# A two-layer mLSTM and conformer trunk on one core: modulation products dealt out, norm 1 without GpSimd, a fourth convolution block on VectorE, and tile starts made equal modulo 64

## The chip, the cores and the metric

The kernel runs on one core of one Trainium2 chip. The metric is the device time of one execution in microseconds; lower is better. Engines are named as in the profile: PE is TensorE (PEld its weight loads), DVE is VectorE, ACT is ScalarE, POOL is GpSimd, SP issues nearly all DMA transfers. Each engine works through its own queue in order.

## The reference

One sequence of 1024 positions and 1024 channels passes two layers. Layer 0 mixes with an mLSTM, layer 1 with a causal conformer convolution; each is followed by a gated ConvFFN (1024 to 2 x 2816 and back). Each sub-layer has a norm that is modulated by a conditioning vector.

```python
c_act = jax.nn.silu(c)
for layer in range(DEPTH):                                   # DEPTH = 2
    mod = c_act @ ada_w[layer] + ada_b[layer]                # 1024 -> 6 * 1024
    sh1, sc1, g1, sh2, sc2, g2 = jnp.split(mod, 6, axis=-1)
    h = modulate(rmsnorm(x, norm_mix_g[layer]), sh1, sc1)
    # layer 0: mlstm_block (w_up 1024 -> 2 * 2048, 4-tap conv, 4 heads, w_down 2048 -> 1024)
    # layer 1: conformer_conv_block:
    #   a, gte = split(h @ w_pw1 + b_pw1); u = a * sigmoid(gte)
    #   u = causal_dwconv(u, dw_w, dw_b)  (31 taps); u = silu(layernorm(u)); y = u @ w_pw2 + b_pw2
    x = x + g1[:, None, :] * y
    h = modulate(rmsnorm(x, norm_ffn_g[layer]), sh2, sc2)
    x = x + g2[:, None, :] * conv_ffn(h, ffn_w_up[layer], ffn_conv_w[layer], ffn_conv_b[layer], ffn_w_down[layer])
return rmsnorm(x, final_g)
```

## The kernel before

**Data and products.** Channels lie on the 128 partitions, positions along the free side, in two halves of 512 (`h` is 0 or 1). A product in fp32 is made of three passes over rounded parts: `split` writes a rounded copy on ACT (L172) and the remainder by a subtract on DVE (L173; on POOL where it is given that engine). `proj` (L201) is one output block of 128 channels for one half: 8 blocks x 3 passes = 24 products. The z half of the mLSTM's up projection and the ConvFFN's matrices use a seven-product form in the manner of Strassen (`Forms`, `Seven`, L468), whose operands are sums of quarters, made on DVE, and whose outputs are combined on DVE and ACT (L564 to L583).

**What sets the order.** A scheduler orders the instructions of each engine from the program's order and priorities and from the tile pools; each engine then runs its queue in order. A tile that is used again makes its next writer wait for its last reader, a DMA writer too.

**The stages** in order of time: norm 1 of layer 0; the x half of the up projection with the 4-tap convolution and the q, k, v maps per block i (16 blocks, `post`); the z half per block j (8); the chunkwise attention; `mlstm_down`, which keeps `residual` steps (L463) for 8 output blocks and both halves and forms the next norm; ConvFFN of layer 0 (up per j, then down); the conformer; ConvFFN of layer 1; the final norm.

**Modulation.** `mod` has 96 columns of 128 channels. Each takes a DMA of 512 KB into a tile `ada` and one DVE operation (`ada_block`, L155: multiply by `crep`, the replicated conditioning vector, and sum), then an add of the bias (L156, one column). 16 of them stand in norm 1, two per i in the x half, ten per j in the z half; all are done before attention. `scale_of` (L161) forms the scale of a norm.

**Norm 1** (`FirstNorm`): the squares of half 0 are summed on PE by a matrix of ones (L310), those of half 1 by adds on POOL (L312) and one product. `apply` scales (L326), maps on ACT (L328, L329) and subtracts (L330), with DVE for half 0 and POOL for half 1.

**The conformer.** `order` gives the projections of pw1. For each block j, `glu` makes the gated u. The blocks j < ON_PE are convolved on DVE (`conv_dve`, L1655: 31 steps of multiply and add, put into a list `slow`, from which `filler(RATE)` takes RATE steps after each projection); the others on PE (`conv_pe`, L1633, with banded weights `wband`, 36 products per half block). For PE's blocks `glu` writes `cU` (L1606), `spread` copies it to `u_d` in DRAM and back as `u`, in four phases. The last four blocks (TAIL) have their projections split by half. `layer_norm` is a generator that `steps` moves on.

Of the kernel before, what the change touches and what calls it, by code (L numbers as in the profile page):

```python
# [15 lines left out]
P = 128  # L16
# [17 lines left out]
EPS = 1e-6  # L34
BIG = 1.0e30
# [31 lines left out]
for _name, _w in (("ident", P), ("posmask", P), ("mask4", 32), ("sel16", 8)):  # L67
    CON[_name] = (_n, _w)
    _n += _w
NCON = _n  # L70
ON_PE = 3
TAIL = 4
LPC = -100
RATE = 5
# [3 lines left out]
def trunk(ctx, tc, a):  # L78
# [50 lines left out]
    epst = main.tile([P, 1], F32, name="epst")  # L129
# [21 lines left out]
    def ada_block(layer, b):  # L151
        crep, pool, bufs = ada_
        w = pool.tile([P, D], F32, tag="ada", name=nm("ada"), bufs=bufs)
        dma(w, a["ada"][layer, b])
        v.scalar_tensor_tensor(w, w, 1.0, crep, ALU.mult, ALU.mult, accum_out=mod[:, layer, b : b + 1])  # L155
        v.tensor_tensor(mod[:, layer, b : b + 1], mod[:, layer, b : b + 1], pv("ada_b", layer, b), ALU.add)  # L156
# [7 lines left out]

    def ada_part(layer, part):
        for k in range(KB):
            ada_block(layer, 8 * part + k)
        if part in (1, 4):
            scale_of(layer, part // 3, 0, KB)
# [129 lines left out]
    class FirstNorm(Norm):  # L299
        def stats(self, h):  # L300
# [5 lines left out]
            for k in range(KB):  # L306
                s = t512()
                sc.activation(s, self.x[:, k, sl], AF.Square)
                if not h:
                    pe.matmul(o, ones, s, start=k == 0, stop=k == KB - 1)  # L310
                elif k:
                    gp.tensor_tensor(acc, acc, s, ALU.add)  # L312
                else:
                    acc = s
            if h:
                pe.matmul(o, ones, acc, start=True, stop=True)
            self.r[h] = inverse_rms(o)

        def apply(self, h, k):
# [6 lines left out]
            (v, gp)[h].tensor_tensor(xs, xs, self.r[h], ALU.mult)  # L326
# [3 lines left out]
            (v, gp)[h].tensor_tensor(hl[:, 1], xs, hl[:, 0].bitcast(F32), ALU.subtract)  # L330
# [116 lines left out]
    def conv_tile(pool, nk):  # L447
        u = pool.tile([P, nk - 1 + S], F32, tag="u", name=nm("u"), bufs=3)
        gp.memset(u[:, : nk - 1], 0.0)
        return u  # L450

    def causal_conv(pool, u, o, h, taps, bias, nk, bufs):
        c0 = h * HS
        sc.copy(u[:, nk - 1 + c0 : nk - 1 + c0 + HS], o)
        c = pool.tile([P, HS], F32, tag="c", name=nm("c"), bufs=bufs)
        sc.activation(c, o, AF.Identity, scale=taps[nk - 1], bias=bias)
        for i in range(nk - 2, -1, -1):
            v.scalar_tensor_tensor(c, u[:, i + c0 : i + c0 + HS], taps[i], c, ALU.mult, ALU.add)
        return c
# [130 lines left out]
    class Operands:  # L590
# [39 lines left out]
        def forms(self, j):  # L630
            b11, b2, t13, t42 = t512(), raw_tile(), raw_tile(self.extra, 2), raw_tile(self.extra, 2)
# [30 lines left out]
    def ffn_up(layer, normed, p_d, hx, ux, es_u, other, ops):  # L662
# [13 lines left out]
        def channel(b, pool=ux):  # L676
            u[b] = pool.tile([P, FK - 1 + S], F32, tag="u", name=nm("u"), bufs=2 + (pool is ux))
# [92 lines left out]
        ops.extra = rx  # L770
# [161 lines left out]
    def mlstm(normed, x0, keep, k1, es1, es_x0):  # L932
# [6 lines left out]
        if True:  # L939
# [4 lines left out]
            g2 = k1.tile([P, IB, 9], F32, name="g2")  # L944
            g1r = k1.tile([P, 2, IB, 8], F32R, name="g1r")
# [8 lines left out]
            ws.load(1, tag="wux", pool=ada_[1], bufs=1, ahead=0, engine=gp)  # L954
            ws.load(lead, ahead=0, engine=gp)
# [37 lines left out]
            ada_[1:] = k1, 2  # L993
            es_x0.close()
            ADAX, ADAZ = 2, 10
            T1_AT, T1_ENG = IB - 2, v
            with ExitStack() as es_z:
# [3 lines left out]
                def post(j, u, xc, xr):  # L1001
# [12 lines left out]
                    bv = mp.tile([P, 137], F32, tag="bv", name=nm("bv"))  # L1014
# [856 lines left out]
```

## Time and profile before

| | us |
|---|---|
| median of 3 runs | 2717.94 (2715.34 to 2719.88) |
| the profiled execution | 2718.93 |
| its span | 2717.0 |

| engine | busy us | share |
|---|---|---|
| PE | 2558.2 | 94% |
| DVE | 2207.1 | 81% |
| ACT | 1353.5 | 50% |
| POOL | 253.5 | 9% |

Stages by the trace: start to 135 us (loads, norm 1, first projections), x half to about 300, z half to 480, attention to 745, mlstm_down to 925, the norm behind it to 991, ConvFFN 0 up to 1372 and down to 1538, conformer to 2016, norm to 2083, ConvFFN 1 up to 2470 and down to 2637, end at 2717. Read the lines so: a group's "mean ns of one" is the duration of one instruction, and the idle time shown with it is that of its engine just before it; a wait's columns are the total, the number and the longest. An engine's idle time matters only where the end of the program hangs on it.

### The profile page before, as it was taken

To read this page: it belongs to the slowest core of one execution; us is meant where nothing else is said; L and a number is where in the kernel's file an instruction comes from. 1 tells how busy PE (TensorE), PEld (TensorE's weight loads), DVE (VectorE), ACT (ScalarE), POOL (GpSimd) and SP (SyncE) were. 2 spreads that over 40 slices of the span, in tenths; PEclk is the share of its full clock that TensorE was granted. 3 is DMA by queue.
4 is the path that set the end of the run, shared out by engine and by line. 5 is a ranking of instruction groups with operands and counts; after the bars stand their busy time and mean duration, and the time that the engine had idled before them with its cause. 6 is when DMAs were issued, how large, how long until landed. Compare 5 with 4: busy or idle time off the path is not lost.

```text
span 2717.0 us, 31936 instructions
## 1 busy us (share of the span) xinstructions
PE 2558.2 (94%) x11565; PEld 2072.4 (76%) x11565; DVE 2207.1 (81%) x3026; ACT 1353.5 (50%) x2085; POOL 253.5 (9%) x338
## 2 busy tenths in 40 slices
PE   4899898999999989999999999799998999999998
PEld 2788676788878768888877888778776788887787
DVE  7999998787767899898898679923489888988866
ACT  4654443777634544444444342466764444445424
POOL 5311254333100000000000000000000000000000
PEclk7999999999999989999999999899998999999999
DMA  7576465532387323233264342444332223326422
GB/s 254 180 244 227 142 209 202 194 119 96 132 282 230 120 101 116 104 110 112 92 219 146 101 144 66 136 159 159 143 119 101 109 102 113 109 89 225 140 80 99
DMA packets 150526, 395.68 MB, mean 146 GB/s; under 512 B 14880, under 2 KB 37600, under 8 KB 150368
## 3 DMA queue, kind: packets, MB, share of 16 engines
q1 hardware_dynamic: 150368, 393.64, 42.2%
q8 instruction: 91, 1.49, 0.2%
q14 instruction: 67, 0.55, 0.1%
HBM read 301.28 MB, written 92.31 MB: 145 GB/s over the span
## 4 chain that ended last, share of the span: by engine, by line
PE 60%; DVE 13%; DMA 4%; ACT 3%; issue 2%; SPq 0%; POOL 0%; DVEq 0%; ACTq 0%; POOLq 0%
PE ps L468 36%; PE ps L201 15%; DVE cy L1655 4%; DVE h L173 3%; PE ps L1381 3%; PE ps L1418 2%; PE ps L1633 2%; DVE wu L173 1%; DVE c L778 1%; DVE x L736 1%; DMA raw<-xc_d 1%; PE ps L1558 1%; DMA raw<-t_d 1%; PE ps L1363 1%; DMA raw<-in_fdownS 0%
## 5 line engine op out<-in xcount | busy, mean ns | idle before, releaser
L468 PE MATMUL ps<-h,wu 128*128 128x512 f32 x4704 | 1121.0, 397 | 42.9 <-ACT wu L172 11.6
L468 PEld LDWEIGHTS ps<-h,wu 128*128 128x128 f32 x4704 | 890.9, 190 | 259.2 <-ACT wu L172 13.7
L201 PE MATMUL ps<-h,wu 128*128 128x512 f32 (+1 forms) x2478 | 574.5, 389 | 1.2 <-DVE wu L173 1.1
L201 PEld LDWEIGHTS ps<-h,wu 128*128 128x128 f32 x2478 | 458.9, 189 | 99.9 <-issue 3.3
L172 ACT CAST wu<-raw 128x1024 fp32r<-128x1024 f32 (+1 forms) x286 | 297.8, 1044 | 285.3 <-PE ps L201 93.4
L173 DVE TENSOR_TENSOR wu<-raw,wu 128x1024 fp32r<-128x1024 f32 (+1 forms) x266 | 322.7, 1214 | 89.2 <-ACT wu L172 88.1
L778 DVE SCALAR_TENSOR_TENSOR c<-u,par,c 128x1024 f32<-128x1024 f32 x176 | 220.9, 1279 | 4.9 <-ACT c L776 4.0
L776 ACT ACTIVATE c<-u,par 128x1024 f32<-128x1024 f32 x88 | 108.9, 1244 | 147.4 <-DVE u L579 130.6
L468 PE MATMUL ps<-h,w 128*128 128x512 f32 x672 | 169.2, 399 | 1.9 <-ACT w L172 1.8
L468 PEld LDWEIGHTS ps<-h,w 128*128 128x128 f32 x672 | 127.5, 190 | 34.0 <-ACT w L172 2.7
L155 DVE SCALAR_TENSOR_TENSOR ada<-ada,crep 128x1024 f32<-128x1024 f32 x96 | 130.6, 1367 | 24.4 <-DMA ada<-in_ada 24.3
L463 DVE SCALAR_TENSOR_TENSOR x<-ps,mod,x 128x512 f32<-128x512 f32 (+1 forms) x140 | 98.0, 714 | 60.0 <-PE ps L201 39.5
L173 DVE TENSOR_TENSOR h<-raw,h 128x512 fp32r<-128x512 f32 (+1 forms) x188 | 124.0, 700 | 25.0 <-ACT h L172 24.8
L172 ACT CAST h<-raw 128x512 fp32r<-128x512 f32 (+1 forms) x188 | 105.8, 606 | 66.7 <-DMA raw<-p_d 26.6
L678 POOL MEMSET u<- 128x2 f32 x88 | 8.5, 100 | 1316.0 <-DVE c L778 716.5
L1381 PE MATMUL ps<-q,h 128*128 128x512 f32 (+2 forms) x576 | 116.0, 350 | 0.3 <-DVE q L173 0.3
L1655 DVE SCALAR_TENSOR_TENSOR cy<-cu,par,cy 128x1024 f32<-128x1024 f32 (+1 forms) x120 | 115.3, 1019 | 1.2 <-ACT cy L1651 0.3
L1633 PE MATMUL ps<-u,wband 128*128 128x128 f32 x720 | 91.3, 293 | 21.0 <-DMA u<-u_d 21.0
L700 ACT ACTIVATE c<-c 128x1024 f32<-128x1024 f32 x44 | 46.7, 1061 | 125.9 <-DVE c L778 125.8
L1633 PEld LDWEIGHTS ps<-u,wband 128*128 128x128 f32 x720 | 90.3, 209 | 23.5 <-issue 20.9
L1381 PEld LDWEIGHTS ps<-q,h 128*128 128x128 f32 x576 | 94.4, 188 | 17.1 <-ACT t L1446 2.0
L1642 ACT ACTIVATE cy<-ps,dwb 32x128 f32<-32x128 f32 x160 | 77.5, 485 | 38.1 <-PE ps L1633 35.8
(272 smaller groups left out, 3371.7 us busy)
## 6 DMA issues: line engine op xcount, KB each, us to landing
ada<-in_ada SPq DMA_DIRECT2D x96, 512.0 KB, 3.9
raw<-in_fup SPq DMA_DIRECT2D x94, 512.0 KB, 3.3
p_d<-c SPq DMA_DIRECT2D x44, 512.0 KB, 2.7
wband<-in_w SPq DMA_DIRECT2D x36, 576.0 KB, 4.7
raw<-in_pw SPq DMA_DIRECT2D x40, 512.0 KB, 3.4
raw<-in_mup SPq DMA_DIRECT2D x32, 512.0 KB, 4.4
raw<-t_d SPq DMA_DIRECT2D x32, 512.0 KB, 4.7
raw<-in_fdownS SPq DMA_DIRECT2D x32, 512.0 KB, 4.3
```

The source lines that it names most:

```text
L155: v.scalar_tensor_tensor(w, w, 1.0, crep, ALU.mult, ALU.mult, accum_out=mod[:, layer, b : b + 1])
L172: sc.copy(out_hi, raw)
L173: (engine or v).tensor_tensor(out_lo, raw, out_hi.bitcast(F32), ALU.subtract)
L201: pe.matmul(o, t[:, i, c : c + P], acts[k][:, j, :], start=k == 0 and n == 0, stop=k == nk - 1 and n == 2,)
L463: v.scalar_tensor_tensor(xs, o, gate, xs, ALU.mult, ALU.add)
L468: pe.matmul(o, w[:, i, k * P : (k + 1) * P], acts[k][:, j, :], start=first and k == 0 and q == 0, stop=last and k == n - 1 and q == 2, ski ...
L776: sc.activation(c, body(b), AF.Identity, scale=taps[FK - 1], bias=pv("fcb", layer, b))
L778: v.scalar_tensor_tensor(c, u[b][:, i : i + S], taps[i], c, ALU.mult, ALU.add)
L1381: pe.matmul(so[:, tlo:], xr[cc][I // nJ][:, i, I % nJ * P : (I % nJ + 1) * P], un["qs"][cc][:, j, tlo:], start=n == 0, stop=n == 3 * CB - 1,)
L1633: pe.matmul(o, wd[:, 4 * d : 4 * d + 4, :].rearrange("p d c -> p (d c)"), phases[j][:, g, n0 + d : n0 + d + N4], start=d == 0, stop=d == 8,)
L1642: sc.activation(y4[32 * g : 32 * g + 32, 3 - q, n0 : n0 + N4], o[32 * q : 32 * q + 32], AF.Identity, bias=dwb4[32 * q : 32 * q + 32, 4 * j ...
L1655: v.scalar_tensor_tensor(y, u[:, t + c0 : t + c1], pv("dww", t, j), y, ALU.mult, ALU.add)
```

## The change

1. **Modulation dealt out.** `ada_product` and `ada_bias` are apart; the bias is added for several columns at once. 16 products stay in norm 1; then 1 per i in the x half, 3 per j in the z half (layer 0's are then done), 28 of layer 1's in `mlstm_down` (one per residual of the stream, 12 in the loop after it, through a single tile), and 20 in ConvFFN 0's up projection (two per j below 4, then one, through the second tile of `ops.extra`; the first holds `crep`, reloaded from DRAM). The pool `m3` has 13 buffers for 15.
2. **Norm 1 and weights without POOL.** Half 1's squares are summed on PE as well, `apply` uses DVE for both halves, and the splits of the first four weights and of the z half's forms j >= 2 move from POOL to DVE.
3. **4-tap convolution** once per block over 1024 columns, after both halves, instead of twice over 512.
4. **Conformer:** ON_PE 4, RATE 6. Blocks 2 and 3 are convolved by halves, their second halves after `filler(-1)`. Each `conv_pe` stands after both projections of the next block instead of between them, and takes one half. `wband` loads are issued by POOL. `layer_norm` yields once more.
5. **Equal offsets:** odd-sized tiles (`epst`, `bv`, `u`, `cu`, `gb2`, `dwb4`, `sel16`) are padded to multiples of 64 bytes, so that all SBUF tiles start at the same place modulo 64.

On PE in the conformer, where the products of block 4, half 0 of the convolution stand (`ps_13505` to `ps_13547` before), between the last products of the first projection of block 5 (`ps_13475`) and the first of its second (`ps_13574`):

```order
L201 MATMUL ps_13475<-h_12548,wu_13425 128x512 x3
L201 MATMUL ps_13475<-h_12553,wu_13425 128x512 x3
L1633 MATMUL ps_13505<-u_1996_13455,wband_13415 128x128 x9
L1633 MATMUL ps_13519<-u_1996_13455,wband_13417 128x128 x9
L1633 MATMUL ps_13533<-u_1996_13455,wband_13419 128x128 x9
L1633 MATMUL ps_13547<-u_1996_13455,wband_13421 128x128 x9
L201 MATMUL ps_13574<-h_12449,wu_13472 128x512 x3
```

After, on PE, the same four stand behind the second projection of block 5 (`ps_13231`), ahead of block 6 (`ps_13343`):

```order
L219 MATMUL ps_13231<-h_12386,wu_13191 128x512 x3
L219 MATMUL ps_13231<-h_12391,wu_13191 128x512 x3
L1644 MATMUL ps_13256<-u_1933_13173,wband_13163 128x128 x9
L1644 MATMUL ps_13270<-u_1933_13173,wband_13165 128x128 x9
L1644 MATMUL ps_13284<-u_1933_13173,wband_13167 128x128 x9
L1644 MATMUL ps_13298<-u_1933_13173,wband_13169 128x128 x9
L219 MATMUL ps_13343<-h_12287,wu_13228 128x512 x3
```

They moved back by one projection of 24 products. On DVE before, the gated tile of block 4, half 0 (`cU_13457`) stands behind the whole of the second block's steps (`cy_12801`, 31 of 1024) and most of what goes with them:

```order
L1655 SCALAR_TENSOR_TENSOR cy_12802<-cu_13066,par,cy_12802 128x512
L1655 SCALAR_TENSOR_TENSOR cy_12801<-cu_12927,par,cy_12801 128x1024
L1606 SCALAR_TENSOR_TENSOR cU_13457<-ps_13273,par,t_1995_13453 128x128x4
L1655 SCALAR_TENSOR_TENSOR cy_12802<-cu_13066,par,cy_12802 128x512
L173 TENSOR_TENSOR wu_13571<-raw_13569,wu_13571 128x1024
L1655 SCALAR_TENSOR_TENSOR cy_12802<-cu_13066,par,cy_12802 128x512 x5
L173 TENSOR_TENSOR wu_13618<-raw_13616,wu_13618 128x1024
L1655 SCALAR_TENSOR_TENSOR cy_12802<-cu_13066,par,cy_12802 128x512 x27
L1606 SCALAR_TENSOR_TENSOR cU_13603<-ps_13475,par,t_2013_13599 128x128x4
```

After, on DVE, `cU_13175` is that tile, and `cy_12639` and `cy_12640` are the second and third block:

```order
L1666 SCALAR_TENSOR_TENSOR cy_12640<-cu_12911,par,cy_12640 128x512
L1666 SCALAR_TENSOR_TENSOR cy_12639<-cu_12768,par,cy_12639 128x1024
L1618 SCALAR_TENSOR_TENSOR cU_13175<-ps_13102,par,t_1932_13171 128x128x4
L1666 SCALAR_TENSOR_TENSOR cy_12639<-cu_12768,par,cy_12639 128x1024
L191 TENSOR_TENSOR wu_13228<-raw_13226,wu_13228 128x1024
L1666 SCALAR_TENSOR_TENSOR cy_12639<-cu_12768,par,cy_12639 128x1024
L1666 SCALAR_TENSOR_TENSOR cy_12640<-cu_12911,par,cy_12640 128x512
```

It stands in the middle of the second block's steps now, with fewer of them ahead of it. On SP in `mlstm_down` after, the modulation tiles stand among the weights (`in_mdown`) and the spilled tiles; before, there are none here:

```order
L156 DMA ada_6319<-in_ada 128x1024
L1497 DMA raw_6436<-hn_d_143 128x512
L200 DMA raw_6446<-in_mdown 128x1024
L1498 DMA raw_6436<-xc_d_111 128x512
L1497 DMA raw_6512<-hn_d_144 128x512
L156 DMA ada_6324<-in_ada 128x1024
L1498 DMA raw_6512<-xc_d_112 128x512
L1499 DMA t_1012_6589<-sz_d_129 128x512
L200 DMA raw_6522<-in_mdown 128x1024
L1499 DMA t_1021_6665<-sz_d_130 128x512
L156 DMA ada_6329<-in_ada 128x1024
```

Each `ada` here writes the tile that the one before it wrote, so what stands behind it on SP waits for the product of the one before.

The diff, cut to its core:

```diff
-ON_PE = 3
+ON_PE = 4
 TAIL = 4
+WIDE = 2
-RATE = 5
+RATE = 6
...
-    epst = main.tile([P, 1], F32, name="epst")
+    epst = main.tile([P, 16], F32, name="epst")[:, 0:1]
...
+    def ada_product(layer, b):
+        crep, take = ada_
+        w = take()
         dma(w, a["ada"][layer, b])
         v.scalar_tensor_tensor(w, w, 1.0, crep, ALU.mult, ALU.mult, accum_out=mod[:, layer, b : b + 1])
+    def ada_bias(layer, b0, b1):
+        ...
+        v.tensor_tensor(m, m, par[:, o + b0 : o + b1], ALU.add)
+    def adas(layer, n):
+        some = blocks_left[layer][:n]
+        del blocks_left[layer][:n]
+        for l, b in some:
+            ada_product(l, b)
+        if some:
+            ada_bias(layer, some[0][1], some[-1][1] + 1)
...
-                if not h:
-                    pe.matmul(o, ones, s, start=k == 0, stop=k == KB - 1)
-                elif k:
-                    gp.tensor_tensor(acc, acc, s, ALU.add)
...
+                pe.matmul(o, ones, s, start=k == 0, stop=k == KB - 1)
...
-            (v, gp)[h].tensor_tensor(xs, xs, self.r[h], ALU.mult)
+            v.tensor_tensor(xs, xs, self.r[h], ALU.mult)
...
-            ws.load(1, tag="wux", pool=ada_[1], bufs=1, ahead=0, engine=gp)
-            ws.load(lead, ahead=0, engine=gp)
+            ws.load(1, tag="wux", pool=xp, bufs=1, ahead=0)
+            ws.load(lead, ahead=0)
...
-                    c = causal_conv(mp, us[i], o, h, taps, pv("mcb", i), MK, 3)
...
+                    sc.copy(us[i][:, MK - 1 + h * HS : MK - 1 + (h + 1) * HS], o)
                     if h == NHALF - 1:
+                        sc.activation(xc, u[:, MK - 1 :], AF.Identity, scale=pv("mcw", MK - 1, i), bias=pv("mcb", i))
+                        for t in range(MK - 2, -1, -1):
+                            v.scalar_tensor_tensor(xc, u[:, t : t + S], pv("mcw", t, i), xc, ALU.mult, ALU.add)
...
-                        adas(ADAX)
+                        adas(0, 1)
...
-                    pairs[j] = Forms(a["mup"][IB + j], a["mup"][IB + KB + j], z1, gp if j >= 2 else None)
+                    pairs[j] = Forms(a["mup"][IB + j], a["mup"][IB + KB + j], z1)
...
-                    if j < KB - 1:
-                        adas(ADAZ)
+                    adas(0, 3)
...
+            if j < FB - 1:
+                adas(1, 2 if j < 4 else 1)
...
-        with phase("m3", 15) as mp:
+        with phase("m3", 13) as mp:
+            crep = mp.tile([P, D], F32, name="crep1", bufs=1)
+            dma(crep, crep_d)
+            ada_[:] = crep, ada_tiles(mp, 1)
...
                 residual(o, gate(i), i, h * HS)
+                adas(1, 1)
...
+                    if m < KB - 2:
+                        adas(1, 1)
...
-                dma(w, a["w4"][j - ON_PE, g])
+                gp.dma_start(w, a["w4"][j - ON_PE, g])
...
-                    us[j] = cp.tile([P, CK - 1 + S], F32, tag="cu", name=nm("cu"), bufs=3)
+                    us[j] = cp.tile([P, S + LINE], F32, tag="cu", name=nm("cu"), bufs=4)
...
                 o = proj(*normed_at(h, n))
                 filler(RATE)
+                og = proj(*normed_at(h, n + 1))
                 while ready:
                     ready.pop(0)()
                 bands(j)
-                og = proj(*normed_at(h, n + 1))
...
                     filler(-1)
-                    slow.append(conv_dve(ON_PE - 1, HS, S))
+                    slow += [conv_dve(i, HS, S) for i in range(WIDE, ON_PE)]
```

More of the change, by code (lines that the diff above doesn't have):

```diff
@@ L149, in raw_tile, with ada_block, ada_tiles @@
         return pool.tile([P, 1024], F32, tag="raw", name=nm("raw"), bufs=bufs)
-    def ada_block(layer, b):
-        crep, pool, bufs = ada_
-        w = pool.tile([P, D], F32, tag="ada", name=nm("ada"), bufs=bufs)
+    def ada_product(layer, b):
+        crep, take = ada_
+        w = take()
         dma(w, a["ada"][layer, b])
         v.scalar_tensor_tensor(w, w, 1.0, crep, ALU.mult, ALU.mult, accum_out=mod[:, layer, b : b + 1])
-        v.tensor_tensor(mod[:, layer, b : b + 1], mod[:, layer, b : b + 1], pv("ada_b", layer, b), ALU.add)
+    def ada_bias(layer, b0, b1):
+        o, _ = PAR["ada_b"]
+        o += 48 * layer
+        m = mod[:, layer, b0:b1]
+        v.tensor_tensor(m, m, par[:, o + b0 : o + b1], ALU.add)
+    def ada_block(layer, b):
+        ada_product(layer, b)
+        ada_bias(layer, b, b + 1)
+    def ada_tiles(pool, bufs):
+        return lambda: pool.tile([P, D], F32, tag="ada", name=nm("ada"), bufs=bufs)
+    blocks_left = [[(0, b) for b in range(16, 48)], [(1, b) for b in range(48)]]
+    def adas(layer, n):
[5 more added lines that the diff above has]
+            ada_bias(layer, some[0][1], some[-1][1] + 1)
     def scale_of(layer, which, k0, k1):
@@ L163, in scale_of @@
         )
[L165 to L169, printed above, removed]
     def split(raw, out_hi, out_lo, engine=None):
@@ L447, in conv_tile @@
     def conv_tile(pool, nk):
-        u = pool.tile([P, nk - 1 + S], F32, tag="u", name=nm("u"), bufs=3)
+        u = pool.tile([P, S + LINE], F32, tag="u", name=nm("u"), bufs=3)[:, : nk - 1 + S]
         gp.memset(u[:, : nk - 1], 0.0)
         return u
[L452 to L459, printed above, removed]
     def residual(o, gate, m, c0):
@@ L769, in ffn_up @@
         rx = es_u.enter_context(phase(nm("rx"), side=other))
-        ops.extra = rx
+        ops.extra = [lambda t=t: rx.tile([P, 1024], F32, tag=t, name=nm(t)) for t in ("ra", "rb")]
+        if blocks_left[1]:
+            ada_[:] = ops.extra[0](), ops.extra[1]
+            dma(ada_[0], crep_d)
         more = single(rx, "w1", 1)
@@ L800, in ffn_up @@
                 s.ready = set()
+            if j < FB - 1:
+                adas(1, 2 if j < 4 else 1)
+                if layer == 0 and not blocks_left[1]:
+                    scale_of(1, 0, 0, KB)
+                    scale_of(1, 1, 0, KB)
             for n, q in enumerate(ORDER):
@@ L944, in mlstm @@
             g2 = k1.tile([P, IB, 9], F32, name="g2")
+            sel16 = k1.tile([P, 48], F32, name="sel16")
+            dma(sel16, a["sel16"])
             g1r = k1.tile([P, 2, IB, 8], F32R, name="g1r")
@@ L1555, in layer_norm @@
                 v.scalar_tensor_tensor(at[j], om, -1.0 / D, at[j], ALU.mult, ALU.add)
+            yield
+            ov = ps()
+            for j in range(KB):
                 t = t512()
@@ L1748, in trunk @@
     x0 = xp.tile([P, KB, S], F32, name="x0")
-    ada_[:] = crep, xp, 5
+    crep_d = dpool.tile([P, D], F32, name="crep_d")
+    dma(crep_d, crep)
+    ada_[:] = crep, ada_tiles(xp, 5)
     for k in range(0, KB, 2):
```

115 lines of the change are left out of this document (50 added, 65 removed).

## The prediction

> **What bounds the kernel now.** I read the page's busy line first, then a table of busy time by stage, then what TensorE (PE) waited for, and last the groups and the timeline in the stages where PE stands.
>
> ```profile
> PE 2558.2 (94%) x11565; PEld 2072.4 (76%) x11565; DVE 2207.1 (81%) x3026; ACT 1353.5 (50%) x2085; POOL 253.5 (9%) x338
> ```
>
> PE is busy 94% of the 2717.0 us span, so almost every microsecond that leaves must be PE work that vanishes, PE work that gets shorter, or one of the few stretches in which PE stands. The table shows where those are (columns: stretch, length, busy time and count of PE, PEld, DVE, ACT, POOL, granted clock, DMA share, GB/s).
>
> ```profile
> 0.00:135.00 135.00, 88.92 (x341) 64.66 (x342) 114.91 (x187) 72.94 (x112) 62.99 (x61) 0.86 0.61 216
> 135.00:300.00 165.00, 164.54 (x815) 138.78 (x813) 158.60 (x344) 82.33 (x146) 33.24 (x58) 1.00 0.71 232
> 300.00:480.00 180.00, 153.40 (x618) 117.66 (x618) 161.95 (x248) 69.31 (x100) 71.45 (x37) 0.95 0.53 182
> 745.00:925.00 180.00, 177.73 (x769) 143.38 (x768) 129.11 (x168) 79.89 (x113) 0.17 (x3) 1.00 0.70 235
> 925.00:991.00 66.00, 51.84 (x195) 37.90 (x193) 59.77 (x83) 36.84 (x55) 0.33 (x4) 0.92 0.16 56
> 991.00:1372.00 381.00, 380.31 (x1656) 312.74 (x1657) 340.88 (x398) 178.83 (x216) 3.71 (x37) 0.99 0.32 114
> 1700.00:1944.00 244.00, 217.72 (x1206) 181.30 (x1204) 113.21 (x136) 150.80 (x267) 0.36 (x4) 0.94 0.46 155
> ```
>
> PE is idle 46.1 us in the start (0 to 135), 26.6 in the z half (300 to 480), 14.2 at the first FFN's norm and 26.3 in the conformer's second part. In the x half (135 to 300) and in the first FFN's up projection it is idle 0.5 and 0.7: there, taking work off VectorE (DVE) is worth nothing. The waits name the releasers.
>
> ```profile
> PE ps L1633 <- DMA u<-u_d: 21.0, 6, 8.9
> PE ps L201 <- ACT h L328: 16.9, 3, 11.7
> PE ps L201 <- DVE h L330: 11.9, 5, 3.1
> PE ps L468 <- DVE zv L571: 10.0, 4, 5.7
> PE ps L310 <- ACT t L308: 9.7, 1, 9.7
> PE ps L468 <- ACT zg L564: 5.3, 2, 3.3
> ```
>
> The first is the conformer's banded convolution, the lines on L201 and L310 are norm 1, those on zv and zg are the z half's combinations.
>
> **Norm 1 without GpSimd (POOL).** The groups give the prices.
>
> ```profile
> L173 POOL TENSOR_TENSOR wu<-raw,wu 128x1024 fp32r<-128x1024 f32 x20 | 55.4, 2780 | 59.6 <-ACT wu L172 59.6
> L326 POOL TENSOR_TENSOR x<-x,t 128x512 f32<-128x512 f32 x8 | 15.9, 2026 | 8.1 <-DVE t L218 8.1
> L330 DVE TENSOR_TENSOR h<-x,h 128x512 fp32r<-128x512 f32 x8 | 10.2, 1270 | 0.0
> L173 DVE TENSOR_TENSOR h<-x,h 128x512 fp32r<-128x512 f32 x56 | 36.3, 683 | 0.0
> L173 DVE TENSOR_TENSOR wu<-raw,wu 128x1024 fp32r<-128x1024 f32 x260 | 317.0, 1220 | 85.3 <-ACT wu L172 84.3
> L1558 PE MATMUL ps<-t,ones 128*128 128x512 f32 x32 | 16.8, 684 | 5.3 <-ACT t L1557 5.3
> ```
>
> One subtract of 512 takes DVE 0.683 us where POOL is quiet and 1.270 in norm 1, where POOL works beside it. The change gives DVE 16 such operations (10.9 us) and about 3 lead weight splits (3.7 us), and takes the interference away: the eight L330 alone get back 8 x (1.270 - 0.683) = 4.7. The second half's statistic becomes seven more fp32 products, 14 records at 16.8/32 = 0.53, 7.4 us of PE, in a stretch where PE stands 46 us. The modulation products of this stage stay 16. From the row of the start, DVE is 85% busy, so more work on it costs the chain unless interference falls by as much. The L156 rows below say that it does. The bounds: nothing (7.4 of PE and 14.6 of DVE eat the relief), and half of the 46.1 idle, since the loads of the first 20 us stay. I take -12, nearer the smaller end, because between 60 and 100 us PE already runs nearly without gaps.
>
> **Modulation and splits in the z half.** Before, ten products L155 with ten adds L156 stand in each j; after, three products and one add.
>
> ```profile
> L155 DVE SCALAR_TENSOR_TENSOR ada<-ada,crep 128x1024 f32<-128x1024 f32 x96 | 130.6, 1367 | 24.4 <-DMA ada<-in_ada 24.3
> 200.00:250.00 50.00, 1.56 (x11) 1.00 0.72 234
> 350.00:400.00 50.00, 8.12 (x12) 0.97 0.60 208
> ```
>
> The last two rows are L156 alone, an add of one column: 0.14 us each in the x half, where POOL does little, 0.68 each in the z half, where POOL splits weights. In a stage row DVE is 90% busy in z. It loses 32 products (48 to 16) at 1.37, 43.7 us, and about 41 adds at 0.14 to 0.68, 6 to 28 us; it gains POOL's splits, 18 x 1.22 + 6 x 0.68 = 26 us, and every remaining operation runs uninhibited. Net -24 to -46 of 162. DVE then is about 70% busy, and the wait for zv (10.0) should go, that for zg (5.3) shrink. PE's idle of 26.6 is the end that the gain can't pass; nothing is the other end, since the splits now stand in DVE's queue ahead of combinations on which PE waits. I take -20: the DVE queue is shortened by more than PE's idle.
>
> On that inhibition the Trainium skill ("SBUF — State Buffer", Two separate sides) says that VectorE and GpSimd take one port pair by an exclusive lock and the loser blocks for the whole instruction. The trace agrees: an add of one column takes five times its time beside POOL. By the rule alone, all of it would vanish with POOL's work; the eight POOL operations on L1056 that stay would keep some.
>
> **The x half.** One product per i instead of two, and the convolution per 1024 columns: all DVE and ACT work under PE that is idle 0.5 us. Taken at nothing; the cover is PE itself. What could cost is that the convolution now starts only after the second half: PE then reads xr later, but one i later anyway. 0 to +5.
>
> **Where the products go.** Of layer 1's 48, 28 move to mlstm_down and 20 to the first FFN's up projection, each with 512 KB.
>
> ```profile
> 770.00:800.00 30.00, 29.49 (x127) 23.21 (x127) 20.52 (x30) 8.90 (x13) 0.00 (x0) 1.00 0.93 329
> ada<-in_ada SPq DMA_DIRECT2D x96, 512.0 KB, 3.9
> wband<-in_w SPq DMA_DIRECT2D x36, 576.0 KB, 4.7
> ```
>
> In mlstm_down DVE has 180 - 129.1 = 50.9 us free; 28 x 1.37 = 38.4 fit, but take most of it. Fourteen MB join some 42 (235 GB/s x 180 us), and at 770 to 800 us the DMA engines are already 93% busy. The products use one tile, so a load on SP's queue waits for the product before it, and the weights and spilled tiles behind it wait too. Bounds: nothing, and 28 x 1.37 if every product lies bare, +38. I take +5 since PE needs some 11 us per residual and a load takes 3.9. The last products fall near the FFN's norm, where DVE is 91% busy: two of them, +3. In the up projection DVE rises from 340.9 by 20 x 1.37 = 27.4 to 368 of 381; the timeline's durations overlap a little, so this is still below full: +1, up to +10. Together +9, 0 to +45.
>
> **The conformer.** One of eight convolution blocks moves from PE to DVE.
>
> ```profile
> L1655 DVE SCALAR_TENSOR_TENSOR cy<-cu,par,cy 128x1024 f32<-128x1024 f32 x60 | 75.2, 1282 | 0.7 <-ACT cy L1651 0.3
> L1655 DVE SCALAR_TENSOR_TENSOR cy<-cu,par,cy 128x512 f32<-128x512 f32 x60 | 42.9, 755 | 0.5
> 1631.72 9.21 DVE L1655 SCALAR_TENSOR_TENSOR cy<-cu,par,cy 128x1024 f32<-128x1024 f32 x7 [0.30 <-ACT cy L1651]
> 1727.30 1.10 DVE L1606 SCALAR_TENSOR_TENSOR cU<-ps,par,t 128x512 f32<-128x512 f32 x1
> 1734.46 18.61 DVE L1655 SCALAR_TENSOR_TENSOR cy<-cu,par,cy 128x512 f32<-128x512 f32 x27
> 1753.00 1.14 DVE L1606 SCALAR_TENSOR_TENSOR cU<-ps,par,t 128x512 f32<-128x512 f32 x1
> 1760.69 4.68 DVE L1655 SCALAR_TENSOR_TENSOR cy<-cu,par,cy 128x512 f32<-128x512 f32 x6
> 1735.34 9.82 PE L1633 MATMUL ps<-u,wband 128*128 128x128 f32 x72 [8.88 <-DMA u<-u_d]
> 1744.91 11.17 PE L201 MATMUL ps<-h,wu 128*128 128x512 f32 x48
> 1760.76 5.46 PE L1633 MATMUL ps<-u,wband 128*128 128x128 f32 x25 [4.68 <-DMA u<-u_d]
> ```
>
> PE loses 144 of 720 records, two pieces like the 72 at 1735.34: 2 x 8 to 9.8 = 16 to 20 us of dense work. The waits before those pieces follow the gated tile cU, written 8 us earlier (1727.30 to 1735.34; 1753.00 to 1760.76), and cU stands late in DVE's queue, full of convolution steps from 1631.72 to about 1765. After, DVE has 60 steps of 512 more, 0.69 each from start to start (27 in 18.61, so each overlaps the next by 0.07), some 41 us, but cU comes with fewer steps ahead of it, and each convolution on PE comes one projection (half of the 11.17) later. Walking the new order from 1631.7 with 1.20 and 0.69 us for steps, 1.14 for a weight split (1.22) and 0.97 for a cU, each less its overlap, the first cU ends at 1708, the tile is there at 1716, and PE wants it at 1720; the next three have 3, 3 and 10 us to spare, and the layer norm's mean finds its blocks at about 1802 where PE gets there at 1795. So all but 5 of the 26.3 idle goes, and 16 of work: -37; with the two transfers at the end of the norm moved earlier, -40. The bounds: -48 (all idle and 20), and -10 (DVE's 41 us push the norm back over most of the gain). I take -40, though the margins are 3 us.
>
> The 32 band loads (36 before) leave SP's queue for POOL's, where no row of before shows a load. SP's other loads only gain by that. SP's 4.7 bounds it below; above, a load has 17.8 us between the last read of its tile and the next need (11.17 for two projections, three quarters of a 9 us piece), so 13 more are free. I take the price as nothing.
>
> **Equal tile offsets.** In the compiled program, 2584 of the 9568 products with 512 columns have their moving and stationary tiles at starts that differ by 32 bytes modulo 64; after, none. The two up projections are the same 1656 products, with 324 such pairs in the first FFN and 719 in the second (L468 alone):
>
> ```profile
> 991.00:1372.00 381.00, 380.31 (x1656) 312.59 (x1656) 0.99 0.32 114
> 2083.00:2470.00 387.00, 385.27 (x1656) 311.50 (x1656) 1.00 0.32 113
> ```
>
> 4.96 us for 395 pairs is 12 ns each. That is an upper estimate, since the stages differ in what runs beside them too; I take half, 6, which also allows for pairs that lie where PE waits. 2584 x 6 is 16: -16, between 0 (the difference has another cause) and -31.
>
> **The sum.** -12 - 20 + 9 - 40 - 16 = -79 on the profiled execution's 2718.93 us: 2640. The median of the runs is 1.0 lower: 2639 us. The likeliest case's own range is 2618 to 2662.
>
> **The rivals.**
> 1. DVE holds the conformer: the margins of 3 us fail, cU stays late in each of the eight half blocks by some 3 us, or the norm waits 20. For it: DVE gets 41 us in the stretch where it has no gap. Against: before, its queue is empty of convolutions from 1765 on while the stage runs to 1944. Then -18 instead of -40: 2661.
> 2. The offsets do nothing: 2655. Against it speak the two equal stages; for it, that they differ in their neighbours as well.
> 3. More is gained: start and z lose all that they can (-23 and -27 instead of -12 and -20) and nothing is paid in mlstm_down: 2612; with offsets at 9 ns too, 2604.
> 4. SP's single tile blocks mlstm_down: every product lies bare there (+38 instead of +5), 2672; with the up projection at DVE's limit (+10), 2681. For it: the 93% above. Against: PE's 11 us per residual.
> 5. Slower: the band loads starve. VectorE runs steps without a gap from 1631 on, and POOL must write these loads' descriptors. If each of the eight half blocks' loads lands later than 4.7 + 13 + 10 = 28 us, PE stands 8 x 10 = 80 us there, and the whole gain is gone; at 35 us each, 2775. For it: POOL's splits took 2.78 where DVE's took 1.22, so POOL does lose to DVE. Against: it lost 1.5 us at a time, not twenty.
>
> The Trainium skill speaks for the fifth ("SBUF — State Buffer", the "DVE blocks DMA" trap): descriptors that GpSimd writes wait while VectorE holds the shared ports. Its own example is a transfer of 620 ns that takes 3100; by that difference each load would come 2.5 us later, inside the slack, and the sum would not move. No trace here shows such a load.
>
> **How the numbers follow.** Forecast 0.50; DVE holds the conformer 0.15; offsets nothing 0.09; more gained 0.12; mlstm_down blocked 0.05; slower 0.06; several terms failing together, near no change, 0.03. The first five are faster by over 0.2% (5.4 us, about what a measurement here can tell from no change): 0.91, of which I give 0.01 to the slower side for terms that I haven't seen: 0.90, 0.03, 0.07. The range runs from the more-gained case, 2604, to the blocked one, 2682.
>
> **What would show it.** The stretch of the conformer from 1700 should be about 205 us of PE with under 8 idle, and waits for u from u_d near zero; L156 at 0.14 us everywhere; PE idle in z under 10; both up projections at one length, near 378; mlstm_down's DMA share up and its PE idle under 8. The prediction is wrong if PE waits for wband, if DVE is full behind 1800, or if SP waits in mlstm_down for the modulation tile while PE stands.

## The result, and the profile after

The changed kernel takes 2656.8 us, median of 4 runs (2656.73 to 2658.55), against 2716.64 (2709.91 to 2719.88) for the kernel before on the same chip: a ratio of 0.9783, 95% interval 0.9768 to 0.9798. The prediction of 2639 was 18 us too low, inside its range of 2604 to 2682. The profiled execution's span is 2655.1 us against 2717.0.

The busy line of the page after, in the same form as the one shown of before:

```profile
PE 2518.8 (95%) x11435; PEld 2054.1 (77%) x11435; DVE 2204.9 (83%) x3055; ACT 1327.5 (50%) x2004; POOL 174.9 (7%) x320
```

PE lost 39 us of busy time; the rest of the 62 us of span is idle time. By stage, with the borders at the first product of each stage in both traces (for mlstm_down at the end of attention's last product):

| stage | before, us | after, us | difference | forecast |
|---|---|---|---|---|
| start and x half, to the first product of z | 285.0 | 270.1 | -14.9 | -12 |
| z half | 203.6 | 173.6 | -30.0 | -20, offsets -2 |
| attention | 252.5 | 252.3 | -0.2 | offsets -3 |
| mlstm_down | 183.7 | 212.5 | +28.8 | +5 |
| norm and ConvFFN 0 | 613.1 | 618.1 | +5.0 | +4, offsets -2 |
| conformer | 478.1 | 438.8 | -39.3 | -40 |
| ConvFFN 1 and the end | 701.0 | 689.7 | -11.3 | offsets -7 |

The large gains came as forecast or larger, and one cost, mlstm_down, was six times its term. (The forecast's offsets, -16, are spread here over the stages by their unequal pairs; the 2 us that are missing lie in the stages with few of them.)

The z half by stage rows, before and after, each from its first product to attention's (length, busy time and count of PE, PEld, DVE, ACT, POOL, granted clock, DMA share, GB/s):

```profile
285.00:488.60 203.60, 176.54 (x720) 136.02 (x719) 182.47 (x290) 80.98 (x121) 77.89 (x40) 0.95 0.55 188
```

```profile
270.10:443.70 173.60, 164.86 (x720) 132.61 (x719) 123.02 (x203) 81.23 (x120) 23.20 (x16) 0.98 0.34 116
```

DVE is 59 us less busy, PE's idle time falls from 27.1 to 8.7, and the same 720 products take 11.7 us less, at a granted clock of 0.98 instead of 0.95 (2 to 3 us of that are the 292 pairs with unequal offsets that stood here). Before, 35 modulation products stood in this stretch:

```profile
L155 DVE SCALAR_TENSOR_TENSOR ada<-ada,crep 128x1024 f32<-128x1024 f32 x35 | 53.0, 1519 | 6.7 <-DMA ada<-in_ada 6.5
```

After, there is none. The program places three in each j, but each engine's order is the scheduler's, and the last product of layer 0 ran at 239 us, in the x half.

What became of the interference shows in the groups of the page after; the bias adds took 377 ns on average before:

```profile
L163 DVE TENSOR_TENSOR mod<-mod,par 128x1 f32<-128x1 f32 x77 | 11.2, 149 | 0.2
L341 DVE TENSOR_TENSOR h<-x,h 128x512 fp32r<-128x512 f32 x16 | 10.5, 683 | 0.8 <-ACT x L340 0.8
L157 DVE SCALAR_TENSOR_TENSOR ada<-ada,crep 128x1024 f32<-128x1024 f32 x76 | 91.6, 1218 | 19.9 <-DMA ada<-in_ada 19.8
```

Norm 1's subtract takes 683 ns instead of 1270, the product 1.22 us instead of 1.37, the add 149 ns.

mlstm_down in two stretches (the sixteen steps of the stream, then the sixteen with gated tiles), first before, then after:

```profile
741.20:836.90 95.70, 91.87 (x391) 72.20 (x390) 67.40 (x90) 40.38 (x58) 0.00 (x0) 1.00 0.79 269
836.90:924.90 88.00, 88.00 (x388) 72.48 (x388) 63.81 (x82) 43.12 (x61) 0.17 (x3) 1.00 0.59 195
```

```profile
696.00:798.00 102.00, 94.44 (x391) 74.29 (x390) 73.03 (x107) 39.44 (x57) 0.00 (x0) 0.97 0.82 278
798.00:908.50 110.50, 96.53 (x388) 75.93 (x387) 90.08 (x143) 44.59 (x62) 0.00 (x0) 0.92 0.76 248
```

In the second stretch PE was never idle before. After, it stands 14.0 us, and its 388 products take 8.5 us longer at a clock of 0.92. The waits in this stage after (from 740 to 908.5 us; for SP, what it stood on):

```profile
ACT wu L190 <- DMA raw<-in_mdown: 36.6, 11, 14.1
PE ps L219 <- ACT wu L190: 12.9, 4, 7.5
SPq L156 <- DVE ada L157: 40.5, 22, 5.6
```

PE waits for a weight's split, the split for the weight's load, and SP, which issues the load, stands 40.5 us on modulation tiles that wait for the product before. In the chain the same names appear: mlstm_down's loads and the modulation tile are in it.

```profile
773.11 5.44 DMA ada<-in_ada
783.82 5.19 DMA raw<-in_mdown
793.23 4.50 DMA ada<-in_ada
```

The two ConvFFNs, whole for ConvFFN 1, before and after:

```profile
2016.00:2636.90 620.90, 600.60 (x2523) 477.88 (x2522) 536.61 (x668) 283.16 (x366) 4.04 (x41) 0.98 0.33 116
```

```profile
1965.30:2575.20 609.90, 588.73 (x2524) 477.46 (x2524) 535.43 (x668) 281.77 (x366) 4.00 (x41) 0.98 0.35 118
```

PE's busy time fell by 11.9 us for the same products at the same clock, with DVE and ACT as before.

### The profile page after: what moved, and what is told of

Same layout as the page of the kernel before. It is cut to its first block, busy times and chain, and to the rows that moved or that the text cites. A ratio compares the mean times of both kernels' runs of the same rounds, so it can differ in the third digit from the quotient of the medians.

```text
span 2655.1 us, 31508 instructions
## 1 busy us (share of the span) xinstructions
PE 2518.8 (95%) x11435; PEld 2054.1 (77%) x11435; DVE 2204.9 (83%) x3055; ACT 1327.5 (50%) x2004; POOL 174.9 (7%) x320
## 4 chain that ended last, share of the span: by engine, by line
PE 64%; DVE 18%; DMA 7%; ACT 6%; issue 3%; POOL 0%; SPq 0%; DVEq 0%; ACTq 0%
PE ps L470 40%; PE ps L219 15%; DVE cy L1666 3%; DVE h L191 3%; DVE wu L191 2%; PE ps L1421 2%; PE ps L1384 2%; DMA raw<-in_mdown 2%; DVE ada L157 1%; DMA ada<-in_ada 1%; ACT cy L1653 1%; PE ps L1644 1%; DMA raw<-xc_d 1%; PE ps L1041 1%; ACT wu L190 1%
## 5 line engine op out<-in xcount | busy, mean ns | idle before, releaser
L470 PE MATMUL ps<-h,wu 128*128 128x512 f32 x4704 | 1106.5, 394 | 37.8 <-ACT wu L190 11.5
L191 DVE TENSOR_TENSOR wu<-raw,wu 128x1024 fp32r<-128x1024 f32 (+1 forms) x286 | 346.9, 1214 | 78.1 <-ACT wu L190 76.5
L1666 DVE SCALAR_TENSOR_TENSOR cy<-cu,par,cy 128x512 f32<-128x512 f32 (+1 forms) x180 | 155.8, 921 | 1.2 <-ACT cy L1662 0.3
L191 DVE TENSOR_TENSOR h<-raw,h 128x512 fp32r<-128x512 f32 (+1 forms) x156 | 102.2, 687 | 22.8 <-ACT h L190 22.6
L190 ACT CAST h<-raw 128x512 fp32r<-128x512 f32 (+1 forms) x156 | 88.8, 604 | 59.6 <-DMA raw<-p_d 26.6
L219 PE MATMUL ps<-go,wu 128*128 128x512 f32 x384 | 96.4, 411 | 14.0 <-ACT wu L190 10.6
L157 DVE SCALAR_TENSOR_TENSOR ada<-ada,crep 128x1024 f32<-128x1024 f32 x76 | 91.6, 1218 | 19.9 <-DMA ada<-in_ada 19.8
L219 PEld LDWEIGHTS ps<-go,wu 128*128 128x128 f32 x384 | 75.6, 199 | 34.5 <-ACT wu L190 11.9
L219 PE MATMUL ps<-h,h 128*128 128x512 f32 (+1 forms) x450 | 83.6, 347 | 0.0
```

Of the source, the lines that this page charges most:

```text
L190: sc.copy(out_hi, raw)
L191: (engine or v).tensor_tensor(out_lo, raw, out_hi.bitcast(F32), ALU.subtract)
L219: pe.matmul(o, t[:, i, c : c + P], acts[k][:, j, :], start=k == 0 and n == 0, stop=k == nk - 1 and n == 2,)
L470: pe.matmul(o, w[:, i, k * P : (k + 1) * P], acts[k][:, j, :], start=first and k == 0 and q == 0, stop=last and k == n - 1 and q == 2, ski ...
L1666: v.scalar_tensor_tensor(y, u[:, t + c0 : t + c1], pv("dww", t, j), y, ALU.mult, ALU.add)
```

## The experiments

All are edits of the changed kernel. Each stage time is from one profile. The stage mlstm_down has the same code in the changed kernel and in five of the experiments; it took 209 to 218 us in these six profiles, so differences of a few us in it are not read. The diffs are cut, and the notes behind # are mine.

**No products in mlstm_down.**

```diff
-                        adas(0, 1)          # x half, per block
+                        adas(0, 2)
-                    adas(0, 3)              # z half, per j
+                    adas(1, 5)
-        with phase("m3", 13) as mp:
+        with phase("m3", 15) as mp:
-                adas(1, 1)                  # both places in mlstm_down, crep's reload with them
```

> The 28 products leave mlstm_down: 32 of layer 0 stand two per i in the x half, 30 of layer 1 five per j in the z half, 18 in ConvFFN 0's up projection, and the pool m3 has 15 buffers again. Changed kernel: 2656.8 us; its stretch from the first product of mlstm_down to the first of ConvFFN 0 took 168.0 us against 141.4 before, and ConvFFN 0's norm some 13 more. If the products there cost that (by whatever way), the stretch is 141 to 144, and the time 2656.8 - 27 - 10 = 2620, up to 2630 if the z half pays for two more products per j. If the loss has another cause in that stage, it stays near 2650.

2632.9 us (2631.88 to 2634.7), ratio 0.9681 (0.9654 to 0.9707): faster than both kernels. mlstm_down took 186.1 us, z 177.0, ConvFFN 0 with its norm 615.0. The second stretch of mlstm_down is again without a gap:

```profile
799.20:887.20 88.00, 88.00 (x388) 72.48 (x388) 64.39 (x83) 43.00 (x61) 0.17 (x3) 1.00 0.62 198
```

So the stage's loss came with the products or with the smaller pool. Z paid 3.4 us for the 20 products that the trace shows in it now, where the changed kernel has none.

**The loads issued by GpSimd.**

```diff
-        dma(w, a["ada"][layer, b])
+        (gp.dma_start if bare[0] else dma)(w, a["ada"][layer, b])   # bare[0] holds in mlstm_down alone
```

> Only the 28 loads of products in mlstm_down are issued by GpSimd and not by SP, same tile, same bytes. Theory queue (SP stands behind a load that waits for its single tile, and the weights behind it come late): the stretch goes from 168 back to 142 to 150, the time to 2630 to 2640. Theory bytes (14 MB more are too many for the DMA engines there): the stretch stays at 165 to 168, the time at 2654 to 2660. Theory VectorE (28 products delay splits): no change either.

2662.7 us (2662.03 to 2666.26); the stage took 217.8. The theory of the queue falls as the only cause: SP no longer stood on these tiles, and nothing came back. (VectorE stood 20.9 us on the loads now, 6.7 in the changed kernel, so this run adds a wait of its own.)

**Products without loads.**

```diff
-        dma(w, a["ada"][layer, b])
-        v.scalar_tensor_tensor(w, w, 1.0, crep, ...)
+        v.scalar_tensor_tensor(w, crep, 1.0, crep, ...)   # in mlstm_down alone
```

> The 28 products in mlstm_down multiply the resident vector with itself, without their loads (layer 1's modulation is then another), so that VectorE's work stays and SP's waits and the bytes go. Queue or bytes: the stretch goes back to 142 to 148, the time to 2625 to 2635. VectorE: it stays at 160 or more, the time above 2648.

2649.6 us (2647.28 to 2653.15), stage 207.1. Neither SP's waits for these tiles nor their bytes can act here, and most of the loss stays. What PE waits for now, from 696 us on:

```profile
PE ps L225 <- DVE wu L197: 7.0, 9, 2.3
PE ps L225 <- ACT wu L196: 6.6, 7, 2.1
```

Sixteen waits of up to 2.3 us each, on the splits of weights. The weights come late here too (the stage's waits of ScalarE, and of SP with the loads of weights):

```profile
ACT wu L196 <- DMA raw<-in_mdown: 38.8, 11, 12.0
SPq L206 <- DVE wu L197: 24.3, 12, 5.1
```

ScalarE stood 38.8 us on them, against 37.1 in the changed kernel and 22.1 before, and SP stood 24.3 us until VectorE had read the tile that a weight was to overwrite, against 9.2 in the changed kernel.

**Loads without products.**

```diff
-        v.scalar_tensor_tensor(w, w, 1.0, crep, ...)
+        v.tensor_copy(mod[:, layer, b : b + 1], w[:, 0:1])   # in mlstm_down alone
```

> The 28 loads stay on SP with their one tile, and instead of the product VectorE copies one column (0.1 us instead of 1.2), so layer 1's modulation is another. Queue: the copy stands at the same place in VectorE's queue, so SP waits nearly as long, and the stretch stays at 158 to 166, the time at 2645 to 2655. Bytes: the same. VectorE: 34 us of work leave, the stretch falls to 145, the time to 2632.

2653.0 us (2646.55 to 2657.14), stage 206.0. VectorE does 24 us less than in the changed kernel (139.2 of 206.0 busy against 163.1 of 212.5), and the loss stays as well. So VectorE's work isn't the only cause either: either half, the loads or the products, is enough to lose most of it. The profiled run was the fastest of the four, 6.5 us under their median, so 206.0 may be low. Here VectorE's small copy stands on its load, with what is queued behind it, and the weights are the latest of all:

```profile
DVE mod L160 <- DMA ada<-in_ada: 12.0, 10, 3.1
ACT wu L195 <- DMA raw<-in_mdown: 48.1, 17, 13.2
```

**No products, but 13 buffers.** The first experiment with `phase("m3", 13)`.

> As the kernel without products in mlstm_down (its stretch from attention's end to ConvFFN 0's first product 186.1 us, 2632.9 us), but with the pool m3 at 13 buffers as in the changed kernel (212.5 us, 2656.8). The runs without loads (207.1) and without products' length (206.0) kept 13 buffers. Theory pool: with 13, five of the second half's gated tiles find a buffer before the first half is done, not seven, and what waits for one blocks its queue: the stretch is 200 to 207, the time 2646 to 2654. Theory products (each of load and product is enough to make the weights late): 186 to 190, 2632 to 2637.

2637.4 us (2633.41 to 2641.9), stage 193.5:

```profile
700.00:798.40 98.40, 91.66 (x391) 72.12 (x390) 66.61 (x89) 40.51 (x58) 0.00 (x0) 1.00 0.76 259
798.40:893.50 95.10, 90.44 (x387) 73.61 (x387) 64.98 (x83) 43.07 (x61) 0.17 (x3) 0.96 0.56 183
```

The smaller pool costs 7.4 us in this profile, 4.6 in the medians, nearly all of it in the second stretch; the products then cost 212.5 - 193.5 = 19. My theory that the pool was most of it falls. With loads alone 12.5 of the 19 are there, with products alone 13.6, each to within the few us that the same code differs by.

**Unequal offsets.** The odd sizes of `epst`, `bv`, `u`, `cu`, `gb2` and `dwb4` as before.

```diff
-    epst = main.tile([P, 16], F32, name="epst")[:, 0:1]
+    epst = main.tile([P, 1], F32, name="epst")
```

> The changed kernel with the odd tile sizes of before (epst, bv, u, cu, gb2, dwb4), so that 1720 of 9568 products with 512 columns have moving and stationary starts that differ by 32 modulo 64; 1212 of them lie in layer 1's ConvFFN and the final stage, as in the kernel before, 400 in ConvFFN 0. Offsets matter: ConvFFN 1's stretch goes from 609.8 back to 620, ConvFFN 0's by 3 to 4, the time from 2656.8 to 2668 to 2674. Offsets do nothing: 2655 to 2659, and the 11 us there had another cause.

2667.6 us (2665.64 to 2671.84), ratio to before 0.9821 (0.9802 to 0.9841) against 0.9783 (0.9768 to 0.9798). ConvFFN 1 took 621.5 us, 11.6 more than 609.9, and ConvFFN 0 1.8 more:

```profile
1964.60:2586.10 621.50, 601.34 (x2524) 478.87 (x2523) 536.77 (x668) 282.95 (x366) 4.00 (x41) 0.98 0.34 116
```

The time of before is back to a microsecond, with its unequal pairs and nothing else of it; in the changed kernel and the other eleven edits ConvFFN 1 took 608.9 to 611.6. PE's busy time grows by 12.6 us for 1105 pairs, 11 ns a pair. ConvFFN 0's 1.8 are not clear of noise: the edits that touch neither it nor mlstm_down took 618.0 to 619.2 there.

**Z's splits on GpSimd.**

```diff
-                    pairs[j] = Forms(a["mup"][IB + j], a["mup"][IB + KB + j], z1)
+                    pairs[j] = Forms(a["mup"][IB + j], a["mup"][IB + KB + j], z1, gp if j >= 2 else None)
```

> The changed kernel with the z half's splits for j >= 2 on GpSimd again, 3 products per j as now. The z half took 203.6 us before and takes 173.6. Interference (GpSimd's splits slow VectorE's operations): 185 to 195, time 2668 to 2678. Products (the 32 fewer products alone shortened z): 172 to 177, time 2654 to 2660.

2667.5 us (2666.69 to 2669.32), z 182.2 us. Both ranges that I gave were missed, in between: 8.6 of the 30 us hang on GpSimd's splits. The other 21.4 stay gained with them there; the 35 products with their adds that left are the main part by size, but the equal offsets are in it too, and no run takes it apart.

```profile
270.10:452.30 182.20, 169.84 (x720) 133.97 (x720) 116.85 (x178) 78.92 (x118) 73.61 (x40) 0.96 0.33 109
```

The same VectorE operation of the z half in this run, then in the changed kernel, shows the interference without any modulation product:

```profile
L525 DVE TENSOR_TENSOR raw<-raw 128x512 f32<-128x512 f32 x7 | 10.6, 1508 | 0.1
L525 DVE TENSOR_TENSOR raw<-raw 128x512 f32<-128x512 f32 x7 | 4.8, 686 | 0.1
```

**Bands by SP.** `dma(w, ...)` for `gp.dma_start(w, ...)` in `bands`.

> The changed kernel with the convolution's 32 band loads on SP's queue again. If GpSimd's descriptor writing made them late, the conformer's 438.8 us shrink by some 5 and the time to 2652. If the slack of 13 us holds, nothing changes, 2655 to 2659. If SP's queue is what the change avoided, the conformer grows by 5 or more, 2662.

2657.8 us (2654.47 to 2660.34), conformer 438.2 against 438.8: no difference. The issue rows of the changed kernel and of this run show what the loads take:

```profile
wband<-in_w POOLq DMA_DIRECT2D x32, 576.0 KB, 5.9
wband<-in_w SPq DMA_DIRECT2D x32, 576.0 KB, 5.3
```

5.9 us to landing from POOL, 5.3 from SP in the same order, 4.7 from SP before.

**Three blocks on VectorE.** ON_PE 3 and RATE 5 in the new order; block 3 goes to the list `ready`.

> The changed kernel with the fourth block's convolution back on PE (ON_PE 3, RATE 5), in the new order otherwise. The conformer took 478.1 us before and takes 438.8. Theory of the prediction (16 to 20 us of PE work from the block, some 20 from waits that the order takes away): 455 to 460, the time 2673 to 2678. Rival (VectorE holds the conformer, so the block's work comes back there): 436 to 445. Third: the order alone did little, 470 or more.

2669.2 us (2666.99 to 2671.8), conformer 446.1: between the first two theories. The new order, with all else that the change does in this stage, is worth 478.1 - 446.1 = 32, the block 7.3. The conformer's middle part with three blocks, then with four:

```profile
1703.00:1900.00 197.00, 192.30 (x1145) 163.28 (x1144) 98.25 (x118) 132.80 (x245) 17.26 (x36) 0.99 0.52 171
```

```profile
1697.00:1885.00 188.00, 177.00 (x1012) 148.20 (x1011) 135.95 (x176) 118.14 (x215) 15.01 (x31) 0.98 0.51 161
```

The fourth block takes 15.3 us of work off PE, and PE's idle time rises from 4.7 to 11.0.

**Norm 1's second half on GpSimd**, with the first four weight splits.

```diff
-            v.tensor_tensor(xs, xs, self.r[h], ALU.mult)
+            (v, gp)[h].tensor_tensor(xs, xs, self.r[h], ALU.mult)
```

> The changed kernel with norm 1's second half (L326, L330 before) and the first four weight splits on GpSimd again; the sum of squares stays on PE. The time to the z half was 285.0 us before and is 270.1. If GpSimd's work is what the change saved there, it goes to 280 to 285, the time to 2667 to 2672. If fewer products and another order did it: 268 to 273, the time 2655 to 2660.

2671.9 us (2669.75 to 2676.26); z began at 286.0 us instead of 270.1. The first 135 us, with GpSimd and without:

```profile
0.00:135.00 135.00, 91.32 (x347) 67.32 (x348) 110.14 (x185) 70.07 (x97) 50.55 (x55) 0.86 0.70 235
```

```profile
0.00:135.00 135.00, 105.18 (x427) 79.22 (x428) 112.78 (x210) 78.33 (x110) 20.18 (x43) 0.91 0.71 242
```

VectorE is about as busy in both, and PE gets through 80 records fewer. The whole gain of the start hangs on GpSimd's work there; the run doesn't tell whether by the interference or because GpSimd's own operations take longer.

**No products in ConvFFN 0 either:** eight per j in z.

> As the kernel without products in mlstm_down (2632.9 us; z 177.0, ConvFFN 0 615.0), and the 18 products of ConvFFN 0 go to the z half too, eight per j. If they cost ConvFFN 0 the 5 us that it is above 609.6 (613.1 before, less 3.5 for the offsets), it goes to 609 to 611; if z then pays nothing, the time is 2628, if z pays 6 to 12, 2633 to 2640. If ConvFFN 0 stays at 615, the products in it cost nothing.

2646.7 us (2643.19 to 2648.38). ConvFFN 0 took 613.3 us for 615.0, z 188.1 for 177.0. The 18 products cost 1.7 in ConvFFN 0 and 11 in z: they stood well. Most of the 11 is one wait for GpSimd at z's end, which neither the kernel before nor the changed one has:

```profile
PE ps L1366 <- POOL ms L1318: 8.9, 1, 8.9
```

**The first experiment with RATE 5.**

> The kernel without products in mlstm_down (2632.9 us, conformer 438.7) with RATE 5: VectorE's queue then holds some 7 steps of 512 fewer (4.8 us) ahead of the gated tile of block 4, half 0, for which PE waits 3.8 us in the changed kernel. If that place is what PE waits for, the wait for u goes and the conformer takes 434 to 436, the time 2629. If the steps only come later at the next place (filler(-1), the norm), 438 to 441 and 2632 to 2636.

2634.2 us (2627.83 to 2636.34), conformer 437.5: no difference from RATE 6 that these runs can tell. The wait for u fell and that for the layer norm's squares rose, first with RATE 6, then with RATE 5:

```profile
PE ps L1638 <- DMA u<-u_d: 4.9, 2, 3.6
PE ps L1564 <- ACT t L1563: 2.3, 3, 1.6
```

```profile
PE ps L1564 <- ACT t L1563: 4.2, 3, 3.6
PE ps L1638 <- DMA u<-u_d: 2.6, 1, 2.6
```

The waits moved to the next place.

## Why the prediction was right, and where it was off

**Start, -12, measured -14.9.** Right in kind: the run with GpSimd's share put back gives all of it back. The bound "nothing (7.4 of PE and 14.6 of DVE eat the relief)" was too careful: VectorE is busy 112.8 of the first 135 us, hardly more than with the 16 operations on GpSimd (110.1), and PE gets further.

**Z, -20, measured -30.0.** The step that failed is "PE's idle of 26.6 is the end that the gain can't pass". Two things pass it. The same products also got shorter, by 11.7 us: 2 to 3 by the offsets, and by the clock, which rose from 0.95 to 0.98, 176.5 x (1 - 0.95/0.98) = 5.4; what is left over stays open. And the idle that I counted was cut at 480 us, 9 us before the stage's end. GpSimd's part is shown, 8.6; the products' part is within the other 21.4. I counted 32 products that leave; the traces show 35 at 1.52 us each, and none left in z. The Trainium skill ("TensorE: Matmul & The Clock Gate", Part 1) says that the clock halves after an idle window of some 3.4 us and comes back after as long a busy one. The rows agree in direction: 1.00 in mlstm_down's second stretch before, where PE never stood, 0.92 after, where it stood 14.0 us, and 0.86 in the first 135 us of the run with norm 1's second half on GpSimd, where it stood 43.7. The windows themselves no row here shows.

**Products elsewhere, +9, measured about +34 (28.8 and 5.0).** This term was mis-sized by some 25 us, more than the whole miss of 18; that start and z gained 13 more than forecast and hid half of it was luck. Its step was "I take +5 since PE needs some 11 us per residual and a load takes 3.9". I weighed one load against one step, as if the stage had room. It had none in any of its parts: DMA engines 59 to 79% busy, SP's queue full of loads that each wait for a tile, VectorE with 51 us free, of which 32 were taken (131.2 to 163.1 us busy), and a pool that lost two of its 15 buffers, which I passed over. The runs price them: pool 5 to 7, products and loads 19 together, and each of the two alone 12 to 14. My own sign of being wrong came: SP waited for the modulation tile there while PE stood. Rival 4 named the place, and its +38 is nearer to 28.8 than my +5, but its mechanism, SP's queue alone, is refuted by the runs with loads from POOL and without loads. What stays open is why each half alone costs more than half of both. The weights land late in all of these runs: without the loads SP stood behind VectorE, without the products VectorE stood on the loads. But that is read from waits, and a run that moves only the products' place in VectorE's queue wasn't made. Since the clock fell to 0.92 there, part of the cost is the same products at a lower clock: 8.5 us of 22.5 in the second stretch.

**ConvFFN 0, +4 less 2 for offsets, measured +5.0.** Its 18 products cost 1.7 in the run that takes them away, near the +1 that I put on 20. The +3 for the norm isn't shown: without products in mlstm_down the stage took 615.0 and 615.3 instead of 618.1, but 617.8 with 13 buffers. Nor are the offsets' 1.8 clear of noise.

**Conformer, -40, measured -39.3.** The total was right, its parts not. That it was right is luck: I put 16 to 20 on the block's work and some 20 on waits; all but the block gave 32, the block 7.3. The block's work did leave PE (15.3 us), but its 41 us on VectorE brought waits back, as rival 1 says: the wait for u before the first piece is 3.78 us where my walk gave 4 to spare, since, counted from the stage's start, PE arrived some 5 us earlier than I had it and the tile 2 to 3 us later. With RATE 5 the steps moved out of the way there, and the stage gained nothing that shows.

```profile
1707.15 9.90 PE L1644 MATMUL ps<-u,wband 128*128 128x128 f32 x72 [3.78 <-DMA u<-u_d]
1729.74 8.28 PE L1644 MATMUL ps<-u,wband 128*128 128x128 f32 x72 [1.75 <-ACT wu L190]
```

**Bands, nothing, measured nothing.** The load takes 0.6 us longer from POOL than from SP in the same order, 1.2 longer than before, within the 13 us of slack. Rival 5 did not come. The Trainium skill's figure, by which I estimated 2.5 us a load ("SBUF — State Buffer", A bandwidth-pool intuition that's wrong), is for a copy on VectorE, which the convolution's steps are not. What the rows show here is a quarter to half of it.

**Offsets, -16, measured -10.8 in the medians** (2667.6 less 2656.8, with 1720 of the 2584 pairs put back; 11.3 were gained in ConvFFN 1 and the end alone). The two up projections that gave me 12 ns hold 240 and 720 such pairs, not 324 and 719, so their 4.96 us are 10 ns a pair. The size of 6 was low for ConvFFN 1 (11 there) and high for a stage's time elsewhere: attention holds 576 pairs and gained 0.2 us, though its products got shorter (last section). Rival 2 is refuted.

## What to carry to other kernels

Price a load or an operation that is moved into a stage by that stage's slack in every queue that it passes (the issuing queue, the DMA engines, VectorE, and the buffers that it takes from others), not by the length of the step beside it; a stage that shows PE without a gap can still have nothing to spare behind it. A stage's idle time isn't the end of what it can gain or lose: here the stretches with gaps also had the lower granted clock, so read busy time, count and clock together. Test the parts of a joined change one at a time even where the sum comes out: here a total of -39.3 against -40 hid two wrong parts, and the best version (2632.9 us) is the change without one of its parts, the products in mlstm_down.

## What the runs showed of the hardware that I had not expected

Products of 512 columns whose moving and stationary tiles start at places that differ by 32 bytes modulo 64 take longer, in every stage that has many of them. Only differences of 0 and 32 occur here. With the tile starts of the compiled program put beside the start times in the traces, the two kinds can be told apart. In the ConvFFN 1 of the run with unequal offsets, the next product starts 234 ns after an unequal one (median of 1058; mean 239) and 229 after an equal one (1351; mean 233). In the changed kernel, where all are equal, it is 227 (2407; mean 230). So an unequal product costs 7 to 9 ns itself, and the rest of the 11 ns falls on the equal ones between.

In attention the medians are 234 before and 227 after. One of its groups, all unequal before and all equal after, in the page's form (a mean duration of 401 and of 397 ns):

```profile
L1381 PE MATMUL ps<-q,h 128*128 128x512 f32 x288 | 72.9, 401 | 0.3 <-DVE q L173 0.3
L1384 PE MATMUL ps<-q,h 128*128 128x512 f32 x288 | 71.8, 397 | 0.4 <-DVE q L191 0.4
```

PE's busy time in that stage fell from 249.3 to 247.4 us, and its idle time grew by nearly as much. The stage's length isn't set by PE's products alone there, so it gained 0.2 us.
